# The first output product of a two-layer trunk in seven block products instead of two passes

## The chip, the cores and the metric

One Trainium2 chip, one of its cores. The metric is the device time of one execution in microseconds, lower is better; a profile of one execution stands beside it.

## The reference

The input x is 1024 tokens by 1024 channels. Two layers follow: a causal convolution mixer and a gated mixer over chunks of 128 tokens. Each widens to 2048 channels, is multiplied with a SiLU gate, and comes back to 1024 channels through `w_out`. That last product is the subject here.

```python
for i in range(DEPTH):                       # DEPTH = 2
    h = _rmsnorm(x, norm_g[i])
    a, b_half, z = jnp.split(jnp.einsum("bsd,de->bse", h, w_in[i]), 3, axis=-1)
    y = conv_mixer(a, b_half, ...) if i == 0 else sgu_mixer(a, b_half, ...)
    x = x + jnp.einsum("bse,ed->bsd", y * jax.nn.silu(z), w_out[i])
    gate = jax.nn.sigmoid(jnp.einsum("bsd,de->bse", _rmsnorm(x, pl_norm_g[i]), pl_gate_w[i]))
    x = x + gate * jnp.einsum("bsk,kd->bsd", p[i], pl_proj_w[i])
return _rmsnorm(x, final_g)
```

In layer 0 the mixer ends in a layer norm over the 2048 channels and a SiLU: y = silu(layernorm(conv)).

## The kernel before

Every float32 product is made of three matmuls: each operand is split into a high part (the value copied to the matmul's format, on ScalarE, names `ahi` and `whi`) and a low part (the value minus the high part, on VectorE or GpSimd, names `alo` and `wlo`), and high x high, high x low and low x high are summed in PSUM. So a tile that is used as an operand costs one copy and one subtraction of 128 x 1024 elements.

The program is written as a list of operations in the order of the computation. A planner then gives each engine its order: it goes through time with an estimated duration for each operation, and each engine takes the ready operation that stands earliest in the program, when buffers for its results are free. Buffers of 4 KB a partition are the pool `w4` (32), weights arrive in `raw` (5) and are split into `whi` and `wlo` (3 each), PSUM has 8 banks of 512 columns. An operation may name a second engine, which takes it when the first is late by a given time: the subtractions go to VectorE, and to GpSimd only when they have been ready for 16 us (`DVE_FIRST`). The result is a fixed order on each engine; nothing is decided at run time.

In layer 0, after the convolution and the statistics of its layer norm (`p_ln0`), `p_g0` describes 16 gated tiles, 8 for each half of 512 tokens, each holding 2 x 128 channels by 512 tokens. A tile is made when it is first asked for (`gate`, L943): load the convolution's result (`gt`) and the SiLU gate (`zt`), subtract the mean and multiply with the inverse deviation, both from PSUM, on VectorE; SiLU on ScalarE (two instructions); multiply with `zt` on GpSimd. In layer 1 the corresponding tiles are complete in memory and are only loaded (`gate`, L1214).

`p_out` (L1002) makes the output product and adds it to the rows of the residual (`xr`). For a layer that isn't in `OUT7` it goes half by half: for each of two column blocks of 512, eight steps over 256 of the 2048 channels (`plain_tok`), each with one weight block of 256 x 512. The splits of activations are kept from the first column block to the second (`sides_of`); the weights are loaded and split for each half again. When a half's rows are complete, `ready` writes them out, normalises them and transposes them for the sigmoid gate's product, `p_gate`.

For a layer in `OUT7` it uses `seven_tok`: the 2048 channels and 1024 columns are cut into 2 x 2 weight blocks, the activations into blocks 11, 12 (half 0) and 21, 22 (half 1), and seven block products take the place of eight, as in Winograd's form of Strassen's scheme. In the chained form that is used here the order is 11, 12, R3, R2, R1, R4, 22, where R3 = 11 - 21, R2 = R3 + 22 with the sign of `once`, and R1 and R4 are differences in the tiles' own place (`once`, L980). A block product has four steps. Sums of weights are made on VectorE or GpSimd from loaded blocks (`add_here`); accumulators are drained and combined between the products:

```python
            for q in range(nq):
                sd = side_of(name, q), split_w(weight(q), shape)
                for t in range(nt):
                    mul(acc[t], t, *sd, first and q == 0, last and q == nq - 1)
```

Of the kernel before, what the change touches and what calls it, by code (L numbers as in the profile page):

```python
# [240 lines left out]
def trunk_kernel(ctx, tc, x, p, norm_g, w_in, w_out, conv_w, conv_b, conv_ln_g,  # L241
# [760 lines left out]
    def p_out(layer):  # L1002
# [18 lines left out]

        if layer in OUT7:
            left = [2 * NT] * 2
# [257 lines left out]
DVE_FIRST = 16000  # L1281
DVE_TAPS = {0: 15}

OUT7 = {1}
O_POOL = None
ALT_ACT0 = 0
PROJ_BACK = 0
# [28 lines left out]
```

## Time and profile before

| | |
|---|---|
| median of 3 runs | 1701.81 us (1701.59 to 1702.53) |
| the profiled execution's own time | 1703.15 us |
| its span | 1701.4 us |
| TensorE matmul, VectorE, ScalarE, GpSimd busy | 96%, 72%, 45%, 42% of the span |
| mean granted clock of TensorE | 0.979 |

The profile names engines PE (TensorE's matmuls), PEld (its weight loads), DVE (VectorE), ACT (ScalarE), POOL (GpSimd) and SP (SyncE). A row of a group gives line, engine, operation, written tile <- read tiles, count, busy time in us with the mean of one in ns, and the engine's idle time before it with what ended that. In the rows of stages the numbers are the stretch in us from the span's start, its length, each engine's busy time with its number of instructions, the granted clock, the share of the DMA engines and GB/s. In the rows in order of time the first two numbers are start and duration, and brackets hold the wait before the instruction. The ends of matmuls are modelled, so their starts are the better measure. A line number can be a helper's: L432 is all split matmuls, L319 and L321 the two-input operations on VectorE and GpSimd, L314 ScalarE's.

### The profile page before, as it was taken

Reading aid. Unit: us, or ns where it says so; the run is one execution under the profiler, and the core shown is the slowest. Engines: PE = TensorE matmul, PEld = TensorE weight load, DVE = VectorE, ACT = ScalarE, POOL = GpSimd, SP = SyncE. Lnnn points to the kernel's source line nnn. Section 1 sums busy time; section 2 is a strip of 40 time slices with the busy share of each in tenths; the row PEclk is TensorE's granted clock in tenths of the full one; section 3 lists DMA queues with packets and bytes.
Section 4 is the critical chain, followed back from the end, with each engine's and each line's share of the span. In section 5 each row is a group of like instructions: output and inputs, shape, how many; then the busy total and the mean of one; then the engine's idle time right before and its main releaser. Section 6 shows DMA issues by size and latency. Waiting matters only on the chain.

```text
span 1701.4 us, 19540 instructions
## 1 busy us (share of the span) xinstructions
PE 1636.0 (96%) x7390; PEld 1349.9 (79%) x7390; DVE 1219.8 (72%) x1304; ACT 758.1 (45%) x944; POOL 712.0 (42%) x420
## 2 busy tenths in 40 slices
PE   6999999999999777999999899999999999999997
PEld 5888888888888655887888688888888888888886
DVE  4399989988989888475355684666666667798655
ACT  6445535445445735264345644333333334333652
POOL 3879999999999926031001411121111110010210
PEclk9999999999999886999999999999999999999999
DMA  5212222222224672483655958676676667845751
GB/s 168 88 62 87 86 76 83 79 75 75 81 85 144 235 241 93 140 291 138 209 199 187 234 148 213 179 173 168 165 180 162 169 164 209 298 161 173 253 216 75
DMA packets 165482, 266.36 MB, mean 157 GB/s; under 512 B 9694, under 2 KB 84558, under 8 KB 165388
## 3 DMA queue, kind: packets, MB, share of 16 engines
q1 hardware_dynamic: 143052, 237.85, 41.5%
q0 software_dynamic: 22336, 27.27, 10.2%
q8 instruction: 58, 0.95, 0.2%
q14 instruction: 36, 0.29, 0.1%
HBM read 206.36 MB, written 58.72 MB: 156 GB/s over the span
## 4 chain that ended last, share of the span: by engine, by line
PE 59%; DVE 1%; POOL 1%; issue 0%; ACT 0%; DVEq 0%; POOLq 0%; ACTq 0%
PE mm L432 41%; PE cv L432 15%; PE mm L1183 1%; PE mm L447 1%; PE cv L1183 0%; PE cv L447 0%; DVE gt L319 0%; DVE xr L319 0%; ACT ahi L314 0%; POOL sm L399 0%; DVE wlo L319 0%; POOL raw L636 0%; PE mm L934 0%; POOL sm L396 0%; DVE alo L319 0%
## 5 line engine op out<-in xcount | busy, mean ns | idle before, releaser
L314 ACT ACTIVATE whi<-raw 128x1024 fp32r<-128x1024 f32 (+1 forms) x198 | 205.9, 1042 | 520.4 <-PE mm L432 246.8
L331 DVE SCALAR_TENSOR_TENSOR cv<-cin,cw,cv 128x1022 f32<-128x1022 f32 (+28 forms) x333 | 423.1, 1271 | 10.0
L432 PE MATMUL mm<-alo,whi 128*128 128x512 f32 x1104 | 429.6, 389 | 0.0
L432 PE MATMUL mm<-ahi,whi 128*128 128x512 f32 x1056 | 413.6, 392 | 0.5 <-DVE alo L331 0.5
L432 PE MATMUL mm<-ahi,wlo 128*128 128x512 f32 x1056 | 411.0, 389 | 0.4 <-POOL wlo L321 0.4
L319 DVE TENSOR_TENSOR wlo<-raw,whi 128x1024 fp32r<-128x1024 f32 x183 | 232.5, 1273 | 161.3 <-ACT whi L314 160.8
L815 POOL TENSOR_TENSOR y<-y,m 128x1023 f32<-128x1023 f32 (+9 forms) x135 | 326.7, 2420 | 12.2 <-ACT m L314 6.1
L432 PE MATMUL mm<-whi,alo 128*128 128x512 f32 x704 | 275.8, 392 | 0.7 <-DVE alo L319 0.7
L432 PE MATMUL mm<-whi,ahi 128*128 128x512 f32 x656 | 258.8, 395 | 6.3 <-ACT ahi L314 5.1
L432 PE MATMUL mm<-wlo,ahi 128*128 128x512 f32 x656 | 257.3, 392 | 3.1 <-DVE wlo L319 3.1
L636 POOL DMA_DIRECT2D raw<-in_w_in_dram x52 | 65.9, 1276 | 427.8 <-DVE wlo L319 258.5
L432 PEld LDWEIGHTS mm<-alo,whi 128*128 128x128 f32 x1104 | 207.3, 188 | 42.5 <-issue 0.5
L432 PEld LDWEIGHTS mm<-ahi,wlo 128*128 128x128 f32 x1056 | 198.2, 188 | 42.1 <-POOL wlo L321 0.9
L432 PEld LDWEIGHTS mm<-ahi,whi 128*128 128x128 f32 x1056 | 198.3, 188 | 41.6 <-ACT whi L314 0.6
L432 PEld LDWEIGHTS mm<-whi,alo 128*128 128x128 f32 x704 | 133.1, 189 | 29.1 <-DVE alo L319 1.4
L432 PEld LDWEIGHTS mm<-whi,ahi 128*128 128x128 f32 x656 | 124.0, 189 | 33.7 <-ACT ahi L314 6.6
L314 ACT ACTIVATE m<-cin,cw 128x1023 f32<-128x1023 f32 (+9 forms) x135 | 147.4, 1128 | 0.0
L432 PEld LDWEIGHTS mm<-wlo,ahi 128*128 128x128 f32 x656 | 124.1, 189 | 29.2 <-DVE wlo L319 3.8
L321 POOL TENSOR_TENSOR wlo<-raw,whi 128x1024 fp32r<-128x1024 f32 (+1 forms) x49 | 109.1, 2229 | 43.0 <-ACT whi L314 40.3
L432 PE MATMUL cv<-whi,ahi 128*128 128x512 f32 x240 | 95.4, 397 | 5.5 <-ACT ahi L314 3.1
L432 PE MATMUL cv<-whi,alo 128*128 128x512 f32 x256 | 100.1, 391 | 0.0
L432 PE MATMUL cv<-wlo,ahi 128*128 128x512 f32 x240 | 94.1, 392 | 0.0
(203 smaller groups left out, 2044.9 us busy)
## 6 DMA issues: line engine op xcount, KB each, us to landing
raw<-in_w_in_dram SPq DMA_DIRECT2D x106, 512.0 KB, 4.1
raw<-in_w_out_dram SPq DMA_DIRECT2D x68, 512.0 KB, 4.6
raw<-in_w_in_dram POOLq DMA_DIRECT2D x52, 512.0 KB, 7.0
raw<-in_pl_gate_w_dram SPq DMA_DIRECT2D x32, 512.0 KB, 4.6
x<-xr SPq DMA_DIRECT2D x24, 512.0 KB, 6.9
xr<-x SPq DMA_DIRECT2D x24, 512.0 KB, 7.4
xr<-in_x_dram SPq DMA_DIRECT2D x16, 512.0 KB, 6.8
yd<-y SPq DMA_DIRECT2D x16, 512.0 KB, 2.9
```

What stands on the lines that cost most here:

```text
L314: nc.scalar.activation(out=o(), in_=i(), func=func, **kw)
L319: dve = (DVE, (150 if ps else 250) + n * 1.042, lambda: nc.vector.tensor_tensor(out=o(), in0=a(), in1=b(), op=alu))
L321: pl = (POOL, 283 + n * 2.06, lambda: nc.gpsimd.tensor_tensor(out=o(), in0=a(), in1=b(), op=alu))
L331: return op(DVE, 214 + n * 1.042, lambda: nc.vector.scalar_tensor_tensor(out=o(), in0=a(), scalar=s(), in1=b(), op0=op0, op1=op1), r, w)
L432: nc.tensor.matmul(out=acc(), lhsT=lw[a](), rhs=rw[b](), start=first and i == 0, stop=last and i == 2, skip_group_check=True)
L447: nc.tensor.transpose(out=ps()[:, t * P:(t + 1) * P], in_=rows[t]()[:, k * P:(k + 1) * P], identity=ident())
L636: op(POOL, 1400, lambda: nc.gpsimd.dma_start(out=raw(), in_=ap(), accum_op=ALU.add), [raw], [raw], size=2 * P * CW * 4)
L815: op(POOL, 283 + CW * 2.06, lambda m=m, s=s: nc.gpsimd.tensor_tensor(out=y()[:, s:], in0=y()[:, s:], in1=m()[:, s:], op=ALU.add), [y, m], ...
L1183: nc.tensor.matmul(out=ps()[:, t * P:(t + 1) * P], lhsT=v()[:, t, j * P:(j + 1) * P], rhs=wT()[:, ct * G // KE, :], start=True, stop=True)
```

## The change

The set of layers whose output product goes by seven block products gets layer 0 as well.

```diff
-OUT7 = {1}
+OUT7 = {0, 1}
```

With it `p_out(0)` takes the branch that `p_out(1)` takes:

```python
        if layer in OUT7:
            left = [2 * NT] * 2
            ...
            seven_tok(once(A), w_out[layer], KE // 4, 0, CB, emit, True, "w4")
            return
```

The tiles that `once` asks for are in layer 0 the callables of `p_g0`'s `gate`, so that the gated tiles of half 0 are made in the first two block products and those of half 1 in the third and fourth (R3 and R2). An activation block that is used in two products is split again for each. The estimates of the planner and all other stages are the same.

## The prediction

> **What bounds the kernel now.** I read the page first, then the busy time of each engine by stage, then the chain that ended last, then the waits and groups of the stage that is changed and of the second output product, which has the new form already.
>
> ```profile
> span 1701.4 us, 19540 instructions
> PE 1636.0 (96%) x7390; PEld 1349.9 (79%) x7390; DVE 1219.8 (72%) x1304; ACT 758.1 (45%) x944; POOL 712.0 (42%) x420
> ```
>
> TensorE is busy nearly throughout, so matmuls saved count in full wherever it stays the last to be ready. The stages of the first output product follow: two column blocks of half 0 (660 to 748), two of half 1 (to 846), then the sigmoid gate's products.
>
> ```profile
> core 0: us, PE busy (x) PEld busy (x) DVE busy (x) ACT busy (x) POOL busy (x), PEclk, DMA share, GB/s
> 636.00:660.00 24.00, 13.84 (x42) 9.21 (x40) 20.52 (x29) 8.59 (x11) 8.37 (x5) 0.50 0.45 160
> 660.00:704.00 44.00, 43.22 (x181) 35.28 (x181) 28.74 (x18) 18.99 (x22) 18.77 (x6) 0.95 0.23 74
> 704.00:748.00 44.00, 44.00 (x194) 36.45 (x195) 26.15 (x25) 16.58 (x20) 8.08 (x4) 1.00 0.67 219
> 748.00:797.00 49.00, 45.49 (x207) 36.41 (x206) 34.00 (x31) 30.14 (x38) 16.48 (x13) 0.97 0.66 231
> 797.00:846.00 49.00, 49.00 (x218) 40.58 (x217) 15.38 (x17) 11.25 (x12) 0.38 (x2) 1.00 0.45 154
> ```
>
> From 660 TensorE is full; VectorE has a third of its time free. Half 1 has the only waits worth counting:
>
> ```profile
> 777.88 0.50 PE L432 MATMUL cv<-whi,ahi 128*128 128x512 f32 x1 [0.78 <-ACT ahi L314]
> ...
> 789.57 0.50 PE L432 MATMUL mm<-whi,ahi 128*128 128x512 f32 x1 [1.19 <-ACT whi L314]
> 790.83 0.80 PE L432 MATMUL mm<-wlo,ahi 128*128 128x512 f32 x1 [0.76 <-DVE wlo L319]
> ...
> 793.56 0.59 PE L432 MATMUL cv<-wlo,ahi 128*128 128x512 f32 x1
> 793.98 0.39 PE L432 MATMUL cv<-whi,alo 128*128 128x512 f32 x1
> ```
>
> The second output product, seven block products, is in these rows (two blocks, R3 and R2, R1, R4, the last):
>
> ```profile
> 1441.00:1485.00 44.00, 44.00 (x196) 36.44 (x195) 32.89 (x32) 17.40 (x19) 0.00 (x0) 1.00 0.86 305
> 1485.00:1529.00 44.00, 44.00 (x196) 36.44 (x195) 41.25 (x38) 17.37 (x17) 5.78 (x2) 1.00 0.48 153
> 1529.00:1551.00 22.00, 22.00 (x99) 18.22 (x98) 18.01 (x19) 8.27 (x8) 0.00 (x0) 1.00 0.56 197
> 1551.00:1573.00 22.00, 22.00 (x99) 18.22 (x98) 19.02 (x21) 8.04 (x8) 0.00 (x0) 1.00 0.51 168
> 1573.00:1599.00 26.00, 25.22 (x128) 20.96 (x127) 19.57 (x26) 16.70 (x23) 5.59 (x8) 1.00 0.58 223
> ```
>
> There the form costs TensorE no wait, but VectorE is at 41.25 of 44 us in the sums R3 and R2, and its tiles come from memory ready made. In the first product VectorE makes them as well. That is the question of this change.
>
> **What is saved on TensorE.** A weight step of the output product is 24 matmuls (4 token tiles, 2 slices, 3 terms):
>
> ```profile
> 704.97 5.45 PE mm L432 x24
> ```
>
> Before, 2 halves x 2 column blocks x 8 steps = 32 steps; after, 7 products x 4 steps = 28. Four steps of 5.45 are 21.8 us. The transposes of the normalised rows and the sigmoid gate's products stay. The waits of half 1 go too, as that pass is gone: 0.78 + 1.19 + 0.76 = 2.7 us, and the seven matmuls from 790.83 to 793.98 took 3.15 us where 7 x 5.45 / 24 = 1.6 is usual: 4.3 us. Together -26.1 us.
>
> **What is added to VectorE.** The prices are in these groups, from 636 to 862 (first four) and from 1434 to 1602 (last four):
>
> ```profile
> L319 DVE TENSOR_TENSOR wlo<-raw,whi 128x1024 fp32r<-128x1024 f32 x33 | 42.9, 1299 | 64.3 <-ACT whi L314 64.2
> L319 DVE TENSOR_TENSOR gt<-gt,mm 128x1024 f32<-128x1024 f32 x32 | 37.7, 1215 | 3.8 <-PE mm L882 2.2 <-PE mm L934 0.8 <-DMA gt<-yd 0.6
> L319 DVE TENSOR_TENSOR xr<-xr,mm 128x512 f32<-128x512 f32 x11 | 7.5, 685 | 3.2 <-PE mm L432 3.2
> L331 DVE SCALAR_TENSOR_TENSOR alo<-mm,gains,ahi 128x512 fp32r<-128x512 f32 x8 | 5.9, 745 | 3.8 <-ACT ahi L314 3.7
> ...
> L319 DVE TENSOR_TENSOR wlo<-raw,whi 128x1024 fp32r<-128x1024 f32 x30 | 36.5, 1221 | 7.0 <-ACT whi L314 6.8
> L319 DVE TENSOR_TENSOR alo<-gt,ahi 128x1024 fp32r<-128x1024 f32 x21 | 25.3, 1220 | 1.5 <-PE cv L432 1.2 <-ACT ahi L314 0.3
> L319 DVE TENSOR_TENSOR gt<-gt,gt 128x1024 f32<-128x1024 f32 x16 | 21.4, 1359 | 3.1 <-DMA gt<-gd 3.1
> L319 DVE TENSOR_TENSOR raw<-raw,raw 128x1024 f32<-128x1024 f32 x14 | 16.8, 1219 | 4.0 <-DMA raw<-in_w_out_dram 4.0
> ```
>
> Added: 16 sums of gated tiles, 16 sums of weights, 12 more activation splits (28 for 16), 20 more drains of accumulators at 0.69; 4 weight splits fewer. At 1.22 each for the large ones that is 40 x 1.22 + 20 x 0.69 = 63 us of VectorE in a stage that becomes 22 us shorter. The 32 gating operations (minus the mean, times the inverse deviation) are unchanged in number, but all 16 tiles are now wanted by the end of the fourth product (R2), at 748 if TensorE never waits; before, half of them were spread to 797.
>
> The product with the SiLU gate runs on GpSimd, and it and VectorE's two-input operations hold each other up:
>
> ```profile
> 636.41 8.01 DVE L319 TENSOR_TENSOR gt<-gt,mm 128x1024 f32<-128x1024 f32 x7 [2.17 <-PE mm L882]
> ...
> 649.11 1.22 DVE L319 TENSOR_TENSOR gt<-gt,mm 128x1024 f32<-128x1024 f32 x1
> 651.17 6.88 DVE L319 TENSOR_TENSOR gt<-gt,mm 128x1024 f32<-128x1024 f32 x6 [0.84 <-PE mm L934]
> 657.97 1.83 DVE L319 TENSOR_TENSOR alo<-gt,ahi 128x1024 fp32r<-128x1024 f32 x1
> ...
> 660.86 2.27 DVE L319 TENSOR_TENSOR alo<-gt,ahi 128x1024 fp32r<-128x1024 f32 x1
> ...
> 664.18 2.29 DVE L319 TENSOR_TENSOR alo<-gt,ahi 128x1024 fp32r<-128x1024 f32 x1
> 668.32 1.50 DVE L319 TENSOR_TENSOR wlo<-raw,whi 128x1024 fp32r<-128x1024 f32 x1 [1.85 <-ACT whi L314]
> 669.74 6.78 DVE L319 TENSOR_TENSOR alo<-gt,ahi 128x1024 fp32r<-128x1024 f32 x2
> 676.44 3.41 DVE L319 TENSOR_TENSOR wlo<-raw,whi 128x1024 fp32r<-128x1024 f32 x1
> ```
>
> ```profile
> L321 POOL TENSOR_TENSOR gt<-gt,zt x16: 2367/2755/3393, 654.0 to 792.0; 128x1024 f32<-128x1024 f32 x16
> ...
> 654.02 24.75 POOL L321 TENSOR_TENSOR gt<-gt,zt 128x1024 f32<-128x1024 f32 x8 [6.52 <-ACT gt L314]
> ```
>
> Seven operations between 657.97 and 679.85 took 18.1 us where 7 x 1.22 = 8.5 would do: 9.5 us lost to eight GpSimd products, 1.2 us each while VectorE is full. The Trainium skill ("SBUF — State Buffer", Who interferes with whom) says that the pair of ports which VectorE and GpSimd share is locked for the whole instruction and the loser blocks; the trace agrees in kind, as the gating operations, with one operand in PSUM, are not lengthened.
>
> **VectorE's account up to R2's last split, from 660.** Gating: 32 less the 14 done by then (7 + 1 + 6) = 18 x 1.22 = 21.9. Activation splits 15 x 1.22 = 18.3 (one was done at 657.97). Weight splits 13 x 1.22 = 15.9 (three are taken as ahead: that many buffers). Sums R3 and R2: 8 x 1.22 = 9.8. Weight sums 8 x 1.22 = 9.8. Four accumulators into rows and four of "d": 8 x 0.69 = 5.5. Lost to GpSimd: 9.5 in the first eight gates as now, and 9.5 for the other eight, since VectorE is now full there too. Sum 100.2 us. The last operands are wanted one step before 748, at 742.6: 82.6 us are there. TensorE waits 17.6 us if VectorE never idles; at the 41.25 of 44 that the second product reached it needs 106.9 us, and the wait is 24. I take 20 between them, because nothing but VectorE is short then: ScalarE has 17.40 + 17.37 us of work in 88 in the second product, and the SiLU adds 32 x 0.80 = 25.6:
>
> ```profile
> L314 ACT ACTIVATE gt<-gt,vec x32: 796/800/814, 652.4 to 791.1; 128x512 f32<-128x512 f32 x32
> ```
>
> R1, R4 and the last product: 8 sums, 12 + 12 splits and 8 weight sums at 1.22 (48.8), 20 drains (13.8), 8 splits of half 0's normalised rows at 0.75 (6.0): 68.6 us of VectorE. TensorE needs 12 x 5.45 = 65.4 and some 4 for transposes, so VectorE no longer falls behind, but it starts with no lead, and "u" and the other drains stand in its queue between splits while the next product waits for the accumulators. The second product has 13 us to spare over these rows (56.6 of 70) and shows no wait; I put 3 us here, between 0 and 8.
>
> The clock: the waits at 789.57 and 790.83 were followed by about 3 us at half speed. The Trainium skill ("TensorE: Matmul & The Clock Gate", What's actually happening) has the clock halve after an idle window of about 3.4 us; no single wait here was that long, so by it short waits cost nothing more, and by the row each such stretch costs 1.7 us. While VectorE is the last, a slower TensorE hides in the same wait, so I add nothing; 0 to 5 is the bound.
>
> Transfers: the added weight loads are 36 for 32 of 512 KB. The second product's first 88 us move 305 and 153 GB/s; the SiLU tiles add 8.4 MB, 95 GB/s, which makes 324 on the mean. That is above the highest row shown, but 160 GB/s flow already before 660 and only 74 from 660 to 704, so there is room to load ahead, and they are taken as hidden. If 305 is the ceiling, 5.5 us come on top. SyncE's queue only issues; four issues more are nothing. GpSimd's queue keeps its 16 products. After the product half 0 is ready one block product (21.8 us) ahead of the end instead of two column blocks, which in the second product was enough: the 1573 row has 25.22 of 26 us busy.
>
> **Sum.** -26.1 + 20 + 3 = -3.1 us. The profiled execution took 1703.15 for a span of 1701.4; the median shown is 1701.81, so the forecast is about 1699 (1700.0 from the profiled time, 1698.7 from the median).
>
> **The rivals.** (a) VectorE keeps up: idle slots such as the 1.85 before 668.32 are filled, weight sums and row additions go to GpSimd, which the planner allows, and gated tiles of half 1 are made in the slack of 660 to 704 (15 us free). Then all waits come to 0 to 6 us: 1676 to 1682. For it: the second product at 94% without a wait. Against: the account is over by 17.6 with no idle time at all.
> (b) Slower: the shared port. If each GpSimd product blocks VectorE for its whole 2.37 (the shortest; 24.75 / 8 = 3.09 with its own waits) instead of 1.2, the 16 cost 38 to 49 instead of 19: the wait is 39 to 50 and the time 1718 to 1729. It decides from a wait of 26.1 - 3 = 23.1 on, or 1.4 us for each product. R3 and R2 bring more two-input work from SBUF for each gating operation than the first eight gates had, so the mean can rise. The Trainium skill's rule of the lock (the same section) would make it the full 38 us wherever nothing else is queued; the 1.2 us measured is half of that. For a middle case I take 1.6 to 1.9, which gives 1705 to 1710.
> (c) The change is not effective: excluded, the branch is taken for every layer in the set.
>
> **How the numbers follow.** Forecast 0.42 (its own range 1693 to 1706), (a) 0.23, (b) 0.35. A measurement of this kernel tells about 0.2% (3.4 us) from no change. Of the forecast 0.20 is faster, 0.15 the same, 0.07 slower; (a) is faster; of (b) 0.04 is the same. So faster 0.43, same 0.19, slower 0.38. The range takes in both: down to the upper part of (a), 1678, and up to the lower end of the full lock, 1718.
>
> **What would show it.** In the changed trace the matmuls stay back to back through the first two block products and then wait in the third and fourth, for VectorE's splits of activations (or ScalarE behind VectorE's sums), 17 to 24 us in all; VectorE is over 90% busy from 660 to about 765; the last row addition of the first product lies near 844 instead of 847.4:
>
> ```profile
> L319 DVE TENSOR_TENSOR xr<-xr,mm x11: 680/686/689, 702.1 to 847.4; 128x512 f32<-128x512 f32 x11
> ```
>
> If VectorE shows idle time in R3 and R2 while TensorE waits, the cause is a chain of loads or tiles not free, and the account is wrong. If TensorE never waits, (a). If split operations average over 1.8 us there, (b).

## The result, and the profile after

The changed kernel takes 1712.69 us (median of 4 runs, 1710.53 to 1714.87) against 1702.17 for the kernel before beside it: ratio 1.0053, 95% interval 1.0037 to 1.0069. It is slower by half a per cent, 13.7 us above the forecast.

The head of the page of the changed kernel, and its stages (the columns as before):

```profile
span 1711.0 us, 19432 instructions
PE 1619.7 (95%) x7294; PEld 1333.8 (78%) x7294; DVE 1288.2 (75%) x1350; ACT 773.3 (45%) x962; POOL 753.4 (44%) x432
```

```profile
660.00:704.00 44.00, 43.31 (x184) 35.41 (x183) 36.75 (x23) 22.57 (x27) 27.59 (x9) 0.96 0.64 216
704.00:748.00 44.00, 26.68 (x100) 19.86 (x98) 43.84 (x31) 16.32 (x18) 26.71 (x9) 0.85 0.35 119
748.00:797.00 49.00, 37.44 (x131) 29.23 (x132) 41.93 (x31) 20.16 (x21) 16.54 (x6) 0.78 0.41 138
797.00:846.00 49.00, 49.00 (x226) 40.84 (x225) 37.18 (x39) 22.88 (x28) 9.95 (x10) 1.00 0.41 141
```

TensorE has 96 matmuls fewer, as foreseen, and loses more than that in the third and fourth block products (704 to 797): 64 of 93 us busy, with VectorE at 43.84 of 44 at first. The transfers are far from full. VectorE is 92% busy from 660 to 765 (96.98 of 105 us). TensorE's waits from 650 to 860, in total, and the single ones after 700 in order of time:

```profile
PE cv L432 <- ACT nhi L314: 14.9, 3, 6.2
PE mm L432 <- ACT ahi L314: 10.3, 2, 5.3
PE mm L432 <- DVE alo L319: 6.5, 3, 4.3
PE cv L432 <- DVE alo L319: 3.2, 1, 3.2
PE cv L432 <- ACT c L314: 0.7, 1, 0.7
```

```profile
706.33 0.50 PE L432 MATMUL mm<-whi,alo 128*128 128x512 f32 x1 [1.46 <-DVE alo L319]
...
721.99 0.80 PE L432 MATMUL mm<-whi,ahi 128*128 128x512 f32 x1 [4.94 <-ACT ahi L314]
722.59 0.63 PE L432 MATMUL mm<-wlo,ahi 128*128 128x512 f32 x1
727.48 0.79 PE L432 MATMUL mm<-whi,alo 128*128 128x512 f32 x1 [4.27 <-DVE alo L319]
...
746.37 0.80 PE L432 MATMUL cv<-whi,nhi 128*128 128x512 f32 x1 [6.24 <-ACT nhi L314]
...
750.79 0.80 PE L432 MATMUL cv<-whi,alo 128*128 128x512 f32 x1 [3.19 <-DVE alo L319]
...
768.13 0.79 PE L432 MATMUL cv<-whi,nhi 128*128 128x512 f32 x1 [4.45 <-ACT nhi L314]
...
780.11 0.80 PE L432 MATMUL cv<-whi,nhi 128*128 128x512 f32 x1 [4.18 <-ACT nhi L314]
```

These seven waits are 28.7 us; all stand in R3 and R2, and all are for an operand made from an activation. The first five (20.1 us) end as soon as VectorE's own operation, or a copy on ScalarE that directly follows one, is done (`nhi` is the copy of a sum). The last two (8.6 us) are another matter, as ScalarE's rows before them and VectorE's last sum before 768.98 show:

```profile
763.72 1.06 ACT L314 ACTIVATE whi<-raw 128x1024 fp32r<-128x1024 f32 x1 [4.31 <-PE mm L432]
764.68 1.99 ACT L314 ACTIVATE ahi<-gt 128x1024 fp32r<-128x1024 f32 x2
767.03 1.06 ACT L314 ACTIVATE nhi<-ahi 128x1024 fp32r<-128x1024 f32 x1 [0.36 <-issue]
...
775.97 1.06 ACT L314 ACTIVATE whi<-raw 128x1024 fp32r<-128x1024 f32 x1 [5.53 <-PE mm L432]
```

```profile
761.86 1.21 DVE L319 TENSOR_TENSOR gt<-gt,gt 128x1024 f32<-128x1024 f32 x1
```

VectorE had the sum ready by 763.07. ScalarE stood still until TensorE's step ended at 763.7, because the next instruction in its fixed order was the copy of a weight block, by its place among the copies the one used two steps later, and that copy waits for TensorE's step to end (`whi` has three buffers). Only behind it came the copies for which TensorE waits at 768.13. At 775.97 it is the same; there VectorE's sum came at 775.86, so about two of the 4.18 us are ScalarE's order (a weight copy and one activation copy that are not wanted yet).

The matmuls after the waits run at half speed: the 231 of 704 to 797 took 64.1 us where 231 x 0.227 = 52.4 is usual, 11.7 us more. The 5.3 in the total is the start of the product, which was there before (5.1). What VectorE and GpSimd did in that time, GpSimd's groups from 650 to 800 and VectorE's from 660 to 800:

```profile
L321 POOL TENSOR_TENSOR gt<-gt,zt 128x1024 f32<-128x1024 f32 x16 | 47.4, 2982 | 53.8 <-ACT gt L314 53.8
L321 POOL TENSOR_TENSOR raw<-raw,raw 128x1024 f32<-128x1024 f32 x10 | 32.4, 3250 | 0.0
```

```profile
L319 DVE TENSOR_TENSOR gt<-gt,gt 128x1024 f32<-128x1024 f32 x16 | 31.8, 1992 | 2.3 <-POOL gt L321 2.3
L319 DVE TENSOR_TENSOR wlo<-raw,whi 128x1024 fp32r<-128x1024 f32 x17 | 31.5, 1853 | 7.1 <-ACT whi L314 7.1
L319 DVE TENSOR_TENSOR alo<-gt,ahi 128x1024 fp32r<-128x1024 f32 x17 | 31.4, 1853 | 0.1
L319 DVE TENSOR_TENSOR gt<-gt,mm 128x1024 f32<-128x1024 f32 x17 | 20.3, 1210 | 0.0
```

The prediction had 16 products on GpSimd. There are 26 instructions: ten weight sums went there too (three expectations below say 11; the rows show ten), by the rule that an operation that has been ready for 16 us may. VectorE's operations on two SBUF tiles took 1.85 to 1.99 us instead of 1.22; those with an operand in PSUM stayed at 1.21. Over the 50 operations of the first three rows that is 16 x 0.77 + 34 x 0.63 = 34 us of VectorE lost, 1.3 for each GpSimd instruction. In order of time on VectorE:

```profile
717.49 3.36 DVE L319 TENSOR_TENSOR gt<-gt,gt 128x1024 f32<-128x1024 f32 x1
720.77 3.38 DVE L319 TENSOR_TENSOR wlo<-raw,whi 128x1024 fp32r<-128x1024 f32 x1
724.08 3.35 DVE L319 TENSOR_TENSOR alo<-gt,ahi 128x1024 fp32r<-128x1024 f32 x1
727.35 3.38 DVE L319 TENSOR_TENSOR gt<-gt,gt 128x1024 f32<-128x1024 f32 x1
730.66 1.21 DVE L319 TENSOR_TENSOR gt<-gt,mm 128x1024 f32<-128x1024 f32 x1
731.79 1.21 DVE L319 TENSOR_TENSOR wlo<-raw,whi 128x1024 fp32r<-128x1024 f32 x1
```

The split that TensorE waits for at 727.48 is the third of these: it and the two before it took 10.1 us where 3.7 would do. The Trainium skill ("SBUF — State Buffer", Who interferes with whom) has the shared ports locked for the whole instruction. These rows agree in kind: each VectorE operation was longer by 2.15 us beside GpSimd instructions of 3.25 on the mean.

**A measure for the experiments.** The planner makes a new order for the whole program at each edit, so totals also move in stages that no edit touches. The "stage" below runs from the start of the first matmul of the first output product to the start of the last row addition of half 1. For the changed kernel it is 655.33 to 859.0 (these rows), 203.7 us; before it was 657.91 to 847.4, 189.5 us.

```profile
655.33 0.79 PE L432 MATMUL mm<-whi,ahi 128*128 128x512 f32 x1 [5.32 <-ACT ahi L314]
```

```profile
L319 DVE TENSOR_TENSOR xr<-xr,u x4: 683/686/687, 855.8 to 859.0; 128x512 f32<-128x512 f32 x4
```

So the product is 14.2 us longer; it starts 2.6 earlier, and the rest of the program is some 2 us shorter, which gives the span's +9.6.

| kernel | weight sums | products with the SiLU gate | stage us | time us | ratio to before, 95% |
|---|---|---|---|---|---|
| before | none | GpSimd | 189.5 | 1702.17 | |
| after | VectorE and GpSimd | GpSimd | 203.7 | 1712.69 | 1.0037 to 1.0069 |
| e1 | VectorE | GpSimd | 187.0 | 1699.37 | 0.9969 to 0.9989 |
| e2 | VectorE and GpSimd | VectorE | 201.3 | 1707.99 | 1.0019 to 1.0043 |
| e3 | adding transfers | GpSimd | 196.5 | 1708.40 | 1.0026 to 1.0050 |
| e6 | GpSimd | GpSimd | 202.8 | 1713.10 | 1.0055 to 1.0079 |
| e5 | VectorE | VectorE | 182.0 | 1691.26 | 0.9927 to 0.9955 |
| e10 | adding transfers | VectorE | 194.8 | 1701.93 | 0.9986 to 1.0008 |
| e11 | 4 adding transfers, 12 VectorE | VectorE | 181.2 | 1690.52 | 0.9913 to 0.9943 |
| e7, two passes as before | none | VectorE | 184.7 | 1701.03 | 0.9984 to 1.0006 |

### The profile page after: what moved, and what is told of

Read it like the earlier page. It is cut to its first block, busy times and chain, and to the rows that moved or that the text cites. A ratio compares the mean times of both kernels' runs of the same rounds, so it can differ in the third digit from the quotient of the medians.

```text
span 1711.0 us, 19432 instructions
## 1 busy us (share of the span) xinstructions
PE 1619.7 (95%) x7294; PEld 1333.8 (78%) x7294; DVE 1288.2 (75%) x1350; ACT 773.3 (45%) x962; POOL 753.4 (44%) x432
## 3 DMA queue, kind: packets, MB, share of 16 engines
q0 software_dynamic: 22336, 27.27, 10.1%
## 4 chain that ended last, share of the span: by engine, by line
PE 56%; DVE 4%; issue 1%; POOL 1%; ACT 0%; DMA 0%; POOLq 0%; DVEq 0%; ACTq 0%
PE mm L432 39%; PE cv L432 14%; DVE gt L319 2%; PE mm L1183 1%; DVE wlo L319 1%; PE mm L447 1%; DVE alo L319 1%; PE cv L1183 0%; DMA raw<-in_w_in_dram 0%; PE cv L447 0%; POOL gt L321 0%; POOL raw L636 0%; POOL sm L399 0%; PE mm L934 0%; POOL sm L396 0%
## 5 line engine op out<-in xcount | busy, mean ns | idle before, releaser
L319 DVE TENSOR_TENSOR wlo<-raw,whi 128x1024 fp32r<-128x1024 f32 x179 | 237.2, 1328 | 110.8 <-ACT whi L314 110.3
L432 PE MATMUL mm<-whi,alo 128*128 128x512 f32 x680 | 268.2, 394 | 6.5 <-DVE alo L319 6.5
L432 PE MATMUL mm<-whi,ahi 128*128 128x512 f32 x608 | 240.5, 396 | 10.3 <-ACT ahi L314 10.3
L432 PE MATMUL mm<-wlo,ahi 128*128 128x512 f32 x608 | 239.0, 393 | 2.3 <-DVE wlo L319 2.3
L432 PEld LDWEIGHTS mm<-whi,alo 128*128 128x128 f32 x680 | 129.6, 191 | 35.4 <-DVE alo L319 8.3
L432 PEld LDWEIGHTS mm<-whi,ahi 128*128 128x128 f32 x608 | 115.3, 190 | 35.7 <-ACT ahi L314 12.0
L432 PEld LDWEIGHTS mm<-wlo,ahi 128*128 128x128 f32 x608 | 115.5, 190 | 26.5 <-DVE wlo L319 2.7
L432 PE MATMUL cv<-whi,ahi 128*128 128x512 f32 x224 | 88.9, 397 | 3.0 <-ACT ahi L314 1.6
L432 PE MATMUL cv<-wlo,ahi 128*128 128x512 f32 x224 | 87.9, 393 | 0.0
```

The costliest lines, as they stand in the source:

```text
L319: dve = (DVE, (150 if ps else 250) + n * 1.042, lambda: nc.vector.tensor_tensor(out=o(), in0=a(), in1=b(), op=alu))
L432: nc.tensor.matmul(out=acc(), lhsT=lw[a](), rhs=rw[b](), start=first and i == 0, stop=last and i == 2, skip_group_check=True)
```

## The experiments

The first theory is the port: GpSimd's instructions hold VectorE up, so taking them off GpSimd makes the kernel faster although VectorE gets more to do. Its rival is the amount: VectorE simply has too much work, and whatever is moved onto it makes it slower. Later a third came in, the order in which the gated tiles are made.

**Which work sits on GpSimd (e1, e2, e6, e5).** e1 keeps the sums of this layer on VectorE:

```diff
-        tt(raw, raw, other, ALU.add, CW, pool=0, r=[raw, other], w=[raw])
+        tt(raw, raw, other, ALU.add, CW, pool=None if st["out"] == 0 else 0, r=[raw, other], w=[raw])
```

> The changed kernel, with the 16 sums of weight blocks of the first output product on VectorE alone (11 of them run on GpSimd in the changed kernel). Theory L (each two-input GpSimd operation holds VectorE up for longer than VectorE would need for the work itself): VectorE gets 11 x 1.22 = 13 us of work and loses some 16 to 22 us less to GpSimd, so 1704 to 1711 against 1712.7. Theory D (only the amount of VectorE's work counts, the lock is small): 13 us more, 1720 to 1726.

(The edits also set `st["out"]` to the layer, a line that is not shown.) Measured: 1699.37, 5 us below the range of Theory L; stage 187.0. That is 16.7 us off the stage for ten instructions moved onto the fuller engine. VectorE's groups in e1, same stretch:

```profile
L319 DVE TENSOR_TENSOR wlo<-raw,whi 128x1024 fp32r<-128x1024 f32 x21 | 29.3, 1397 | 5.7 <-ACT whi L314 5.7
L319 DVE TENSOR_TENSOR alo<-gt,ahi 128x1024 fp32r<-128x1024 f32 x17 | 26.1, 1539 | 1.0 <-ACT ahi L314 0.9
L319 DVE TENSOR_TENSOR raw<-raw,raw 128x1024 f32<-128x1024 f32 x12 | 24.3, 2028 | 0.0
L319 DVE TENSOR_TENSOR gt<-gt,mm 128x1024 f32<-128x1024 f32 x17 | 20.6, 1209 | 0.0
L319 DVE TENSOR_TENSOR gt<-gt,gt 128x1024 f32<-128x1024 f32 x16 | 20.3, 1281 | 0.0
```

By the same reckoning 21 x 0.18 + 17 x 0.32 + 12 x 0.81 + 16 x 0.06 = 20 us are lost, 1.2 for each of 16 products: the prediction's price, in a kernel with the prediction's work.

e2 is the other half: the products on VectorE, the sums as the planner likes.

```diff
-            tt(g, g, z, ALU.mult, CW, pool=0, r=[g, z], w=[g], pool_first=True)
+            tt(g, g, z, ALU.mult, CW, r=[g, z], w=[g])
```

> The changed kernel, with the 16 products with the SiLU gate on VectorE instead of GpSimd. Theory L: VectorE gets 16 x 1.22 = 19.5 us of work, 16 to 25 us of waits for GpSimd go (weight sums may still go to GpSimd): 1706 to 1715. Theory D: 15 to 20 us slower, 1727 to 1733.

Measured: 1707.99, in the range of Theory L, but the stage is 201.3, hardly shorter than after's. GpSimd did ten instructions now, nine sums and one weight split. By VectorE's durations these cost it only some 10 us, so this run does not fit the port's account alone. Its trace shows what holds TensorE instead, in three waits of R2 (3.80, 4.45 and 3.52 us); the first one, with ScalarE's and VectorE's rows:

```profile
754.24 0.79 PE L432 MATMUL cv<-whi,nhi 128*128 128x512 f32 x1 [3.80 <-ACT nhi L314]
```

```profile
750.54 1.06 ACT L314 ACTIVATE whi<-raw 128x1024 fp32r<-128x1024 f32 x1 [7.04 <-PE mm L432]
751.50 1.04 ACT L314 ACTIVATE ahi<-gt 128x1024 fp32r<-128x1024 f32 x1
```

```profile
752.57 1.23 DVE L319 TENSOR_TENSOR alo<-ahi,gt 128x1024 fp32r<-128x1024 f32 x1 [3.29 <-ACT ahi L314]
```

VectorE has time here and waits itself (3.29, 3.58 and 5.00 us) for ScalarE's copy, and ScalarE stands behind the copy of a weight that is used two steps later, until TensorE's step ends. The last two waits in the changed kernel are of this kind. It is read from the trace; no run changes ScalarE's order. e6 puts every sum on GpSimd:

```diff
+        if st["out"] == 0:
+            op(POOL, 283 + CW * 2.06, lambda: nc.gpsimd.tensor_tensor(out=raw(), in0=raw(), in1=other(), op=ALU.add),
+               [raw, other], [raw], port=True)
```

> The changed kernel with all 16 weight sums of the first output product on GpSimd (11 in the changed kernel, none in the one at 1699.4). Theory L: from 0 to 11 the price was 13 us and the last row addition moved from 841.5 to 859.0, so 1.2 to 1.6 us a sum; five more: 1717 to 1722, last row addition at 864 to 868. Theory D: five sums less on VectorE, 6 us faster, 1705 to 1709.

Measured: 1713.10, stage 202.8, as after; neither range was met. Six sums more on GpSimd made no difference, so the price isn't one for each instruction. e5 takes both off GpSimd (the edits of e1 and e2):

> The changed kernel with both the weight sums of the first output product and the products with the SiLU gate on VectorE alone. Against the kernel with only the weight sums there (1699.4; its last row addition of the first product starts at 841.5), VectorE gets 16 x 1.22 = 19.5 us more and is spared the 24 us that its two-input operations still lose to 16 GpSimd products. Theory L (the port): 1693 to 1700, last row addition at 835 to 842. Theory D (amount of VectorE's work): 1712 to 1720, last row addition at 855 to 861.

Measured: 1691.26, just below the range of Theory L; stage 182.0, faster than before by 0.6%. Its stages:

```profile
704.00:748.00 44.00, 31.39 (x117) 23.82 (x116) 43.70 (x42) 20.55 (x24) 0.00 (x0) 0.90 0.43 143
748.00:797.00 49.00, 47.39 (x204) 38.47 (x203) 46.71 (x45) 22.98 (x23) 4.41 (x2) 0.98 0.50 171
```

and those of e1:

```profile
704.00:748.00 44.00, 32.28 (x116) 23.32 (x114) 43.74 (x37) 21.08 (x24) 13.44 (x5) 0.88 0.36 120
748.00:797.00 49.00, 45.25 (x184) 36.51 (x185) 46.47 (x43) 21.48 (x22) 10.44 (x4) 0.93 0.50 172
```

Counted over 704 to 797, VectorE and GpSimd together finish 62 + 15 = 77 instructions in after, 80 + 9 = 89 in e1, and 87 + 2 = 89 in e5, where GpSimd does next to nothing. TensorE gets 231, 300 and 321 matmuls in. The second engine added nothing to the work done in these 93 us; with sums on it as well, less was done (e6: 61 + 16 = 77 again). A part of the 77 is idle time: VectorE stood still for 7 us of the 93 in after, for 3 in e1 and e5. What is shown is that the sums on GpSimd cost the stage 16.7 us (after against e1) and 19.3 us (e2 against e5), and that VectorE's operations grow beside them; that the port is all of it is not shown, and e2 speaks against it.

**Is it the amount of work? (e4, e8, e9).** e4 leaves out the mean's subtraction (16 operations of 1.22, 19 us), everything else as after:

```diff
-            tt(g, g, wide(mean), ALU.subtract, CW, True, r=[g, mean], w=[g])
```

> The changed kernel without the subtraction of the mean in the gated tiles of layer 0 (part of the computation left out), so 16 x 1.215 = 19.4 us less on VectorE, none of which shares a port with GpSimd. Theory that VectorE is the bound of the first output product (L and D alike): 12 to 20 us faster, 1693 to 1701. Rival: TensorE waits for the length of the chain load, gate, sum, split with tiles not free, not for VectorE's amount: less than 6 us faster, 1707 or more.

Measured: stage 203.4, unchanged, on the rival's side. Its time, 1731.45, is no measure of the edit: a stage that the edit doesn't touch became longer. From 1180 to 1380 TensorE was busy for all 200 us before, and in e4:

```profile
1180.00:1380.00 200.00, 191.69 (x905) 157.57 (x904) 121.06 (x182) 60.58 (x75) 24.74 (x19) 1.00 0.68 161
```

(many waits of up to 0.8 us for drains of accumulators; why the new order brings them is open.) e8 leaves the weight sums out, with the products on GpSimd; e9 also has the products on VectorE.

```diff
-        tt(raw, raw, other, ALU.add, CW, pool=0, r=[raw, other], w=[raw])
+        if st["out"]:
+            tt(raw, raw, other, ALU.add, CW, pool=0, r=[raw, other], w=[raw])
```

> The changed kernel without the additions of the weight sums in the first output product (the blocks are loaded, the additions left out, part of the computation left out). Against the one with the sums on VectorE (1699.4, last row addition at 841.5) 19.5 us of VectorE's work are gone. If VectorE is what TensorE waits for, sums and lock: last row addition at 826 to 834, 1684 to 1692. If the length of the chain load, gate, product, sum, split or free tiles are: 838 or later, 1696 or more.

> The kernel with both kinds of products on VectorE (1691.3, last row addition of the first output product at 837.5, VectorE without a gap from 698 to 784), with the additions of the weight sums in that product left out (part of the computation left out). With GpSimd on the gate products the same omission moved the last row addition from 841.5 to 843.9, that is not at all, with VectorE idle for 7 to 8 us in each stretch. Theory V (without GpSimd's operations the amount of VectorE's work is the bound): 16 x 1.22 = 19.5 us less work, last row addition at 820 to 826, about 1674 to 1681. Theory C (the chain from load over gate and sum to split is the bound in both): 833 or later, 1687 or more.

Measured: e8 1696.06, stage 189.9, longer than e1's although 16 operations are gone; e9 1691.46, stage 181.2, as e5. Both are what the expectations gave for the length of the chain (load, gate, sum, split), not for the amount. VectorE is not full in e8 (37.02 of 44 us, then 41.17 of 49) and TensorE waits all the same. Between e5 and e9 GpSimd plays no part; 16 x 1.22 = 20 us of VectorE's work go and nothing is gained: something else sets the end as well.

**Transfers that add (e3, e10, e11).** In e3 the second weight block is added by the transfer that loads it, not by an engine; e10 is e3 with the products on VectorE.

```diff
-              lambda raw, q, kh, n: add_load(raw, ap(q, kh, n)) if hold == "raw" and not SUM_B or not SUM_W else add_here(
+              lambda raw, q, kh, n: add_load(raw, ap(q, kh, n)) if hold == "raw" and not SUM_B or not SUM_W or st["out"] == 0 else add_here(
```

> The changed kernel, with the 16 sums of weight blocks of the first output product made by transfers that add to the tile, issued from GpSimd's queue, so that neither VectorE nor GpSimd computes them. Theory L: 5 sums leave VectorE (6 us) and 11 GpSimd operations with their 16 to 22 us of waits go: 1688 to 1698. Theory D: only the 6 us of VectorE go: 1705 to 1709. A rival to both: the adding transfers land late behind GpSimd's products in its queue, and the matmuls wait for them: 1710 or more.

> The gate products on VectorE and the weight sums of the first output product by adding transfers from GpSimd's queue. VectorE and GpSimd are as in the run without weight sums. Theory V, if the transfers come in time: last row addition at 822 to 830, 1676 to 1684. Theory T (the adding transfers are slow: with GpSimd's gate products the DMA engines were at 0.90 of their time at 231 GB/s between 704 and 748, and matmuls waited for weights): 845 to 855, 1699 to 1709.

Measured: e3 1708.40, stage 196.5; e10 1701.93, stage 194.8, as Theory T had it. They free VectorE (37.06 of 44), and against e1 and e5 the stage is 9.5 and 12.8 us longer. The stage and the largest single wait of e10:

```profile
704.00:748.00 44.00, 29.18 (x108) 22.46 (x107) 37.06 (x35) 17.76 (x20) 9.69 (x8) 0.81 0.90 215
```

```profile
PE mm L432 <- ACT whi L314: 9.1, 1, 9.1
```

TensorE now waits for weights, which come late: the DMA engines are 0.90 busy at 215 GB/s, where plain loads showed 0.86 at 305. In e3, whose time lies in the range of Theory D, it is the third theory too: 9.4 us of waits are for weights. Not all of e10's loss is the transfers': 9.6 us more of waits are for `nhi`, two of the three behind ScalarE's order as in e2. e11 lets only the first four sums be made so:

> The gate products on VectorE, the first four weight sums (for R3) by adding transfers, the other twelve on VectorE. Against the kernel with all on VectorE (1691.3, last row addition at 837.5) 4 x 1.22 = 4.9 us less of VectorE's work ahead of R3. Theory V with transfers in time: 831 to 835, 1685 to 1689. Theory T: 838 or later, 1691 or more.

Measured: 1690.52, stage 181.2, between the two ranges. Its interval overlaps with e5's, so the four adding transfers make no difference that is shown.

**Free tiles (e12, e13).** e12 is e5 with 34 large tiles; to make room `raw` has 4 buffers and another pool 12 instead of 14. e13 is the control with those two alone.

```diff
-W4_BUFS = 32
+W4_BUFS = 34
-S2_BUFS = 14
-RAW_BUFS = 5
+S2_BUFS = 12
+RAW_BUFS = 4
```

> Both kinds of products on VectorE, with 34 instead of 32 of the large tiles (w4), paid for by 12 instead of 14 of the half tiles (s2) and 4 instead of 5 buffers for weights (raw). If too few free large tiles delay the loads of half 1's gated tiles: last row addition of the first output product 3 to 8 us earlier than in the run with the same half tiles and weight buffers and 32 large tiles. If not: within 2 us of it.

> Control for the run with 34 large tiles: both kinds of products on VectorE, 32 large tiles, 12 half tiles, 4 weight buffers. Expected at 837.5 (as with 14 and 5) to 843 if the weight buffers were needed.

Measured: stages 184.6 and 183.2 (times 1727.69 and 1691.56; e12 loses its time outside the stage, a good part of it where e4 does). Two tiles more don't help, so the number of tiles is not shown to be a limit.

**How far the form itself goes (e15, e14).** Both start from e5. e15 loads the gated tiles and leaves out all that is done to them; e14 leaves out the product with the SiLU gate and its load.

> Weight sums on VectorE, gated tiles of layer 0 only loaded: mean, deviation, SiLU and gate product left out (part of the computation left out), as the second output product has it. The form itself then costs TensorE no wait: 28 steps of 5.45 us, 152.6, from a first matmul near 650, and transposes: last row addition at 808 to 818. If TensorE still waits in R3 and R2, the form and not the gating is at fault: 825 or later.

> Weight sums on VectorE, the products with the SiLU gate and the loads of it left out (part of the computation left out). Against both on VectorE (last row addition at 837.5): 19.5 us of VectorE's work less, one large tile less for each gated tile while it is made, the chain shorter by one step. Leaving out the weight sums, also 19.5 us, moved it by 1.6 only. If free tiles or the length of the chain hold TensorE: 822 to 831. If neither, 834 to 838.

Measured: e15 1680.28, e14 1678.33. In e15 the last row addition starts at 823.1, between the two ranges and 14.4 us before e5's, and TensorE's waits from 650 to 860 are 2.9 us in all, the longest 1.4. So without the gating nothing of the trouble in R3 and R2 is left, though every sum, split and drain of the form is there. How long the form takes by itself e15 doesn't tell: its tiles need no statistics of the layer norm, so the whole first block product (96 matmuls) ran already between 583 and 625,

```profile
583.60 0.49 PE L432 MATMUL mm<-whi,ahi 128*128 128x512 f32 x1 [0.28 <-ACT whi L314]
```

and 63 matmuls of another product ran after 670. The 152.9 that the next expectations name is the time from 670.2 to 823.1; that it lies near 28 x 5.45 = 152.6 is chance. e14's stage is 171.3, 10.7 less than e5's, in the range given for free tiles or the length of the chain.

**The order (e16, e17).** The 16 sums could be left out for nothing, the 16 products not. The tiles of half 1 are asked for only in R3, so they stand late in the planner's list, behind all earlier work. e16 is e5 with the gating of half 1 placed 60 (shown) or 150 operations earlier in the list; e17 has the 60 and leaves out the sums.

```diff
+                    back = 60 if st["out"] == 0 and n[0] == "2" else 0
+                    plan.offset -= back
                     A[n][q] = A[n][q]()
+                    plan.offset += back
```

> Both kinds of products on VectorE; the operations of half 1's gated tiles get a priority 60 operations earlier in the planner's order, about three weight steps. From the first matmul to the last row addition the stage took 182.0 us with both on VectorE, 152.9 with tiles only loaded. If the chain of gating is begun too late: 170 to 178. If VectorE simply has no time earlier, or the gates push out the splits of the first two products: 180 to 186.

> The same with 150 operations, about seven weight steps. If the chain is begun too late: 166 to 178 for the stage. If early gates push out the splits of the first two products: more than 182, with waits of TensorE between 660 and 704.

> Products with the SiLU gate on VectorE, half 1's gating 60 operations earlier in the planner's order, and the additions of the weight sums left out (part of the computation left out). Each alone did nothing for the stage: earlier gating 182.9 against 182.0 us with VectorE full from 704 to 748 and the waits gone over to the weight sums, sums left out 181.2 with gaps on VectorE. If two limits lie on top of each other (VectorE's amount of work, and gating that the planner's order begins late): 167 to 175 us for the stage, about 1677 to 1684 in all. If another link of the chain holds: 179 or more.

Measured: 1690.67 (stage 182.9), 1694.62 (186.6) and, without the sums, 1680.15 (171.2). The earlier order alone gains nothing, the smaller amount alone (e9) gains nothing, both together take 10.8 us off e5's stage. The stage of e17:

```profile
704.00:748.00 44.00, 40.85 (x162) 32.49 (x163) 43.77 (x42) 25.14 (x28) 0.00 (x0) 0.92 0.37 129
```

VectorE does 42 operations in these 44 us as in e5, at the same 43.7 us, but without a weight sum among them, and TensorE gets 162 matmuls in for 117. Two limits stood at nearly the same place, and each hid the other.

**Before, with the products on VectorE (e7).** It is the kernel before with e2's edit:

> The kernel before the change with the 16 products with the SiLU gate on VectorE instead of GpSimd. There VectorE has a third of its time free, and loses 14 us to GpSimd in the whole stage. Theory L: waits hurt only where VectorE is full, here from 652 to 687, so at most 3 us faster or slower, 1699 to 1705. A rival, that the products on GpSimd cost much before the change too: 1695 or less.

Measured: 1701.03, stage 184.7. The old form too gains 4.8 us in this stage when GpSimd is left out, and the waits of half 1 are gone; 11 us are then lost later, a part of them from 1180 to 1380, where e4 loses too (the profiled execution is e7's slowest, 1705.01). Between the two forms, both without GpSimd, lie 182.0 and 184.7: seven products gain 2.7 us here, not the 21.8 of their matmuls. Most of what e5 gains in the stage is gained by either form.

## Why the prediction was wrong

**The saving** was right: 96 matmuls fewer, and the waits of half 1 gone.

**Where the waits come** was right: back to back through products 11 and 12, then waits in R3 and R2 for activation splits and for copies behind VectorE's sums, but for the last two, which stand behind ScalarE's order. The tail was put at 3 us; after 786 there is 0.7.

**The size of the wait** is what failed: "I take 20". Measured were 28.7 us of waits and 11.7 at half speed after them, 40.4 together, against 20 and 0 in the sum; with the saving and the tail, -26.1 + 40.4 + 0.7 = 15.0, and the stage is 14.2 longer. Three steps of the prediction lie behind it.

First, "GpSimd's queue keeps its 16 products" and "Weight sums 8 x 1.22 = 9.8" on VectorE. Ten sums went to GpSimd, and "lost to GpSimd" is 34 instead of 19. e1, with the sums kept on VectorE, gives 16.7 us of the stage back. The rule of 16 us was in front of me; the sums are loaded early and wanted late, so they are the first to be ready that long. But the account itself doesn't make 16.7 of it: with the division as it was it becomes 100.2 - 9.8 + (34 - 19) = 105.4 of 82.6 available, a wait of 22.8 with no idle time and of 30 at the 41.25 of 44 used before. That leaves 10 to 18 us of the 40.4.

Second, "nothing but VectorE is short then". ScalarE has time, but its order is fixed, and the last two waits (8.6 us) stand behind its copy of a weight for a later step, the second of them only in part. The price of that is not tested.

Third, the clock, which follows below.

The kernel for which the account was made is e1: sums on VectorE, 16 products at 1.2 each. It took 1699.37 for the 1699 forecast, and its last row addition started at 841.5 for the 844 named. That looks like a proof of the account, but is luck in part: e8 leaves 16 sums out of e1, and its stage is 2.9 us longer where the account makes it shorter by some 10.

**Rival (a)** counted the sums' going to GpSimd in its favour. The runs show the opposite: e1 against after is 16.7 us of stage for keeping them away.

**Rival (b)** names the mechanism that VectorE's rows show, with the wrong cause of its size; the time lies between its middle case (1705 to 1710) and the full lock (1718). The price did not rise much (1.3 for 1.2, still under the deciding 1.4); the number rose, 26 for 16. The sign that the prediction named for (b), splits over 1.8 us on average, is there from 660 to 800 (1.853); in R3 and R2 alone, 704 to 790, the 21 splits average 1.79.

**The clock** was put at 0, "0 to 5 is the bound", as "a slower TensorE hides in the same wait". Most of the 11.7 us did: had TensorE been faster there, it would have reached the next late operand earlier and waited longer. After the wait at 780.11 no wait follows that would hide it: the matmuls start 0.43 us apart until 786.26, 13 of them in 6.15 us where 13 x 0.227 = 3.0 is usual, so 3.2 us came on top, inside the bound. This is read from the trace and not tested.

**What the account never had** is the order. It added up work against time, as if VectorE always did the most urgent thing. e8 and e9 against e17 show that this was a limit of its own, at about the same height. ScalarE's order is part of it, as the waits of e2 show. Why e4 gains nothing is open; neither was run with another order.

**The transfers** were rightly taken as hidden: no TensorE wait is for them, and they run at 119 to 216 GB/s.

## What to carry to other kernels

Before a two-input operation is given to a second engine that shares ports with a full first one, count what both finish together: here 77 instructions with more on GpSimd, 89 with less and 89 with almost none. With a fixed order on each engine, look also at what stands in front of the urgent operation: a copy for later that waits for a buffer held up the engine that was to free it. A fallback rule such as "the other engine takes what has waited long" picks the work that is least urgent and lets it hold up the most urgent; ask which operations will meet the rule before adding any. When an edit that removes work gains nothing, another limit may stand at the same height: try the two together (e17), and judge by the stage, since the rest of the program moved by up to 28 us (e12 against before) from a new order alone. Check first that the stage begins with the same work: in e15 it did not.

## What the runs showed of the hardware that I had not expected

In these 93 us VectorE finished as much alone (e5) as together with GpSimd (e1), with most operations on two SBUF tiles. The Trainium skill ("GPSIMD Engine Reference", 4.1 Engine selection) gives two-input elementwise work to VectorE because GpSimd takes about twice as long; the trace agrees (2.37 us at best against 1.22), and adds what the first engine loses, 1.2 to 1.3 us each time.

Transfers that add, in the mix of this stage, cost the DMA engines more than their bytes say: 0.90 busy at 215 to 231 GB/s (e10, e3), where plain loads showed 0.86 at 305.

The clock: in the changed kernel matmuls ran 0.43 us apart after the waits of 3.19 (right behind that of 6.24) to 6.24 us (granted clock 0.50 from 728 to 731 and from 780 to 786), and at their usual 0.23 after that of 1.46 at 706.33. That goes with the window of 3.4 us in the Trainium skill ("TensorE: Matmul & The Clock Gate", What's actually happening) better than the kernel before did, where 1.19 and 0.76 us were enough.
